# Layer-norm statistics by one product with a constant matrix, and attention that forms three heads' scores ahead

## The chip, the cores and the metric

The kernel runs on one core of one Trainium2 chip. The number that counts is the device time of one execution in microseconds (us). The engines are TensorE (PE in the profile, with its weight loads as PEld), VectorE (DVE), ScalarE (ACT), GpSimd (POOL) and SyncE (SP); SP only issues the DMAs that bring weights in.

## What is computed

The reference is a decoder trunk of two layers over 256 tokens of width 2048, in float32: a gated short convolution with an MLP, then latent attention (16 heads, keys and values from a shared latent of 512) with an MLP, and a layer norm behind each of the four.

```python
def layer_norm(x, g, b):
    mu = jnp.mean(xf, axis=-1, keepdims=True)
    var = jnp.mean(jnp.square(xf - mu), axis=-1, keepdims=True)
    y = (xf - mu) * lax.rsqrt(var + LN_EPS) * g + b
...
    s = (einsum(qn, k_nope) + einsum(qp, k_pe)) * scale    # per head and block of 128 queries
    p = jax.nn.softmax(jnp.where(mask, s, -inf))
    return einsum(p, v)
...
        h = layer_norm(ALPHA * h + mix, ln_g[layer, 0], ln_b[layer, 0])
        h = layer_norm(ALPHA * h + sq_relu_mlp(h, ...), ln_g[layer, 1], ln_b[layer, 1])
```

## The kernel before

Activations lie with the model dimension on the 128 partitions: `xres[:, m, :]` is chunk m of 16, 128 features by 256 tokens. Weights come from HBM in pieces of 512 KB (`raw` or `w`). ACT rounds such a piece to `hi` (a cast to fp32r), DVE forms the remainder `lo<-raw,hi`, and PE multiplies by both: two products with `hi`, one with `lo`. So nearly every weight piece costs an ACT instruction of about 1.05 us and a DVE instruction of about 1.2 us besides its products.

**Layer norms.** The class `Norm` (line 379) handles the first three norms: index 0 ahead of the first MLP, 1 ahead of the attention, 2 ahead of the second MLP. The fourth norm is done token by token at the end and is not touched. `prepare` and `count` sum the chunks and their squares into `S` and `Q`, 128x256 each: what is left is a sum over the partitions. The products that follow don't wait for the norm. They are taken on the not yet normalised input (`xd`), and the result is corrected with `A` (the reciprocal standard deviation of a token) and `B` (minus mean times `A`), both spread over all partitions as 128x256. `weighted` does this correction; on DVE it shows as `t<-ps_g,ab` or `t<-ps_w,ab`. `normal(m)` makes chunk m's normalised value for the residual path: two DVE instructions `nu` and one ACT instruction.

`stats` and `finish` make `A` and `B`. Four products with `S` or `Q` as weights and one column `col` as the moving side give the mean and the mean square of 128 tokens each, with tokens on partitions (`stat`, 128x4). Eight DVE instructions on 128x2 and a square root on ACT follow (`nm`, `ve` twice, `iv`, `rt`, `ra`, `rr`, `nr`). Four PE transposes by the identity `id_t` spread the two results to `lnAB`, and two ACT copies bring them to `ab`.

**Attention.** `wide_products` (line 1168) yields the nine products of the latents and calls `finish` of norm 1 first; after each of them but the first, it makes one `normal`. `project(g, box)` makes keys (`ps_k`), values (`ps_v`), rotary queries (`ps_p`) and queries (`ps_q`) of a group of four heads, in 12 steps, and two `normal` at its end. `attend(h, box)` is one head in three steps: scores `S` with mask, maximum, exponential, sum and scaling on DVE and ACT; three transposes `tp` with a copy `pt`; the product `po` with its split into `oT`. The loop behind them alternates one step of `attention` of the group before and one step of `project` of the group that follows (for the last group, of the output projection `ps_wo`). The order of the heads' steps is fixed by hand in `attention` (line 1287). Scores lie in two PSUM buffers `S`, `tp` and `po` in one each, the probabilities of a head in one of two buffers `pr2`.

The framework orders instructions of each engine on its own; only the instructions inside the MLPs' planned part keep their program order. So the place of an instruction follows from the order in the program and from the framework's scheduler. Nearly every instruction carries line 71 of the helper that records it; the names of the tiles tell them apart.

Of the kernel before, what the change touches and what calls it, by code (L numbers as in the profile page):

```python
# [53 lines left out]
def trunk(ctx: ExitStack, tc: tile.TileContext, opening, xT, vecs, w_in, w_out, w_kv, w_q, w_uk, w_uv,  # L54
# [299 lines left out]
    for _ in range(WARM):  # L354
        tensor.matmul(warm[:, :P], ones, ones, start=True, stop=True)
    vector.memset(col[:, 0:1], 1.0 / D)
    vector.memset(col[:, 1:2], 1.0 / RK)

# [20 lines left out]
    class Norm:  # L379
# [3 lines left out]
        def __init__(self, idx, scale):  # L383
            self.idx, self.scale = idx, scale
            self.S = act.tile([P, T], F32, tag="S", name=f"S{idx}")
            self.Q = act.tile([P, T], F32, tag="Q", name=f"Q{idx}")
            self.mu0 = act.tile([P, T], F32, tag="mu0", name=f"mu0{idx}") if idx != 1 else None
            self.ws = None

        def means(self):  # L390

            ps = psum("mu0c")
            for t in range(2):
                tensor.matmul(ps[:, t:t + 1], xres[:, 0, t * P:(t + 1) * P], ones[:, 0:1], start=True, stop=True)
            self.off = small.tile([P, 2], F32, tag="nm", name="off")
            vector.tensor_scalar(self.off, ps[:, 0:2], -self.scale, None, ALU.mult)
# [42 lines left out]

        def stats(self):  # L440

            st = psum("stat")
            for j in range(2):
                for b in range(2):
                    c = st[:, 2 * j + b:2 * j + b + 1]
                    tok = slice(b * P, (b + 1) * P)
                    tensor.matmul(c, (self.S, self.Q)[j][:, tok], col[:, 0:1], start=True, stop=True)
            nm = small.tile([P, 2], F32, tag="nm", name="nm")
            vector.tensor_scalar(nm, st[:, 0:2], -1.0, None, ALU.mult)
            ve = small.tile([P, 2], F32, tag="ve", name="ve")  # L450
            vector.tensor_tensor(ve, nm, nm, ALU.mult)
            vector.scalar_tensor_tensor(ve, st[:, 2:4], LN_EPS, ve, ALU.add, ALU.subtract)
            r = small.tile([P, 2], F32, tag="rr", name="rr")
            rsqrt(r, ve)
            return nm, r

        def finish(self):
            nm, r = self.stats()
            n = small.tile([P, 2], F32, tag="nr", name="nr")
            vector.tensor_tensor(n, nm, r, ALU.mult)  # L460
            ps = psum("lnAB")
            spread(ps[:, :T], r)
            spread(ps[:, T:], n)
            ab = act.tile([P, 2 * T], F32, tag="ab", name=f"ab{self.idx}")
            scalar.copy(ab[:, :T], ps[:, :T])
            scalar.copy(ab[:, T:], ps[:, T:])
            self.A, self.B = ab[:, :T], ab[:, T:]

        def gain(self, m):
# [649 lines left out]
    with tc.tile_pool(name="att", bufs=1) as ap:  # L1119
# [35 lines left out]
        def rms(out, sqs):  # L1155

            st = psum("rstat")
            for b in range(2):
                tensor.matmul(st[:, b:b + 1], sqs[:, b * P:(b + 1) * P], col[:, 1:2], start=True, stop=True)
            ve = small.tile([P, 2], F32, tag="ve", name="rve")  # L1160
            vector.tensor_scalar(ve, st[:, 0:2], RMS_EPS, None, ALU.add)
            rsqrt(out, ve)

        csq = act.tile([P, T], F32, tag="S", name="csq")
        qsq = act.tile([P, T], F32, tag="Q", name="qsq")
        todo = iter(range(NC))

        def wide_products():
            ln.finish()
            for i in range(2 * NK + 1):  # L1170
                if i < GROUP:
                    ps = ln.ws[i][1]
                else:
                    ps = psum("ps_w")
                    mm_wide([(take(), ps)], ln.xd)
                if i:
                    ln.normal(next(todo))
                yield ps
# [27 lines left out]
        oT = [ot[:, k, :] for k in range(H)]  # L1206
        kq, vp = (array(a, F32, f"kqv{a}", NC * W) for a in ("a1", "a2"))
        k2, q2, v2 = ([r[:, o:o + 1024].rearrange("p (j t) -> p j t", j=J) for o in (b, b + 1024)]
                      for r, b, J in ((kq, 0, 4), (kq, 2048, 4), (vp, 0, 2)))
        p2 = [vp[:, o:o + 512].rearrange("p (j t) -> p j t", j=2) for o in (2048, 2560)]  # L1210
        pr2 = [vp[:, o:o + 3 * P] for o in (3072, 3456)]

        with tc.tile_pool(name="att2", bufs=2) as a2, \
                tc.tile_pool(name="paux", bufs=1, space=PS) as paux:
            def project(g, box):
# [28 lines left out]
                if g == 0:  # L1244
                    query_scale()
                for _ in range(2):
                    ln.normal(next(todo))

            def attend(h, box):
# [6 lines left out]
                for b, (at, n) in enumerate(spans):  # L1256
                    tok = slice(b * P, (b + 1) * P)
                    tensor.matmul(S[:, at:at + n], qn[:, tok], kn[:, :n], start=True, stop=False)
                    tensor.matmul(S[:, at:at + n], qp[:, tok], kp[:, :n], start=False, stop=True)
                pr = pr2[h % 2]  # L1260
                mx = small.tile([P, 2], F32, tag="mx", name="mx")
# [25 lines left out]
            def attention(g, box):  # L1287
                gens = [attend(4 * g + j, box) for j in range(4)]
                for step in range(6):
                    for j in range(3, -1, -1):  # L1290
                        if 0 <= step - j < 3:
                            next(gens[j])
                            yield

# [165 lines left out]
```

## Time and profile before

| | |
|---|---|
| median of three runs | 1992.5 us (1992.46 to 1992.79) |
| the profiled execution | 1992.93 us, its span 1991.1 us |
| granted TensorE clock, mean | 0.998 |
| PE, PEld busy | 1978.0 us (99%), 1734.7 us (87%) |
| DVE busy | 1742.3 us (88%) |
| ACT busy | 1390.7 us (70%) |
| norm 0, 1, 2: first `stat` product | 380.1, 1058 and 1321 us from the span's start |
| attention, groups 0 to 3 | from 1114.6 to 1229 us |

The time of the execution is 1.8 us over the span, which goes from the first to the last instruction. A timeline's row has the start, the duration and the instruction; an "x" behind it means that some of one kind are merged, and the bracket tells how long the engine stood idle before it and on whom it waited. The durations of PE's instructions overlap, since matmuls are pipelined: what a product costs is the distance between starts.

### The profile page before, as it was taken

The page shows a single profiled execution, that of the slowest core. Times are in us where ns is not written, and L with a number is a line of the kernel's source. Part 1 is how long each engine was busy: PE and PEld are TensorE (multiplying, and loading weights), DVE is VectorE, ACT ScalarE, POOL GpSimd, SP SyncE. Part 2 cuts the span into 40 slices and gives each one's busy share as a digit, 9 for nine tenths or more (in the row PEclk, how much of TensorE's full clock was granted, in tenths as well). Part 3 has the DMA queues.
Part 4 walks back from the last instruction along what each step waited for, and adds up shares of the span by engine and source line. Part 5 has one row for each costly group of instructions (what it writes and reads, how often), then busy time and mean ns, then how long its engine had stood idle before and what let it go on. Part 6 is the DMA issues. An engine that isn't in the chain of part 4 may idle for free.

```text
span 1991.1 us, 29733 instructions
## 1 busy us (share of the span) xinstructions
PE 1978.0 (99%) x11058; PEld 1734.7 (87%) x11058; DVE 1742.3 (88%) x2630; ACT 1390.7 (70%) x2069; POOL 2.3 (0%) x21
## 2 busy tenths in 40 slices
PE   9999999999999999999999999999999999999997
PEld 8888888988888888888889998898888888888886
DVE  7657567789999999999988978778999999999997
ACT  6444445577888788878857655557788788887871
POOL 0000000000000000000000000000000000000000
PEclk9999999999999999999999999999999999999999
DMA  9655555556666666666765543654666666666673
GB/s 333 232 184 191 190 185 195 161 162 196 204 203 207 204 202 207 203 202 206 222 210 164 159 126 118 202 169 154 201 201 205 200 208 203 203 208 201 201 249 110
DMA packets 107858, 387.39 MB, mean 195 GB/s; under 512 B 11969, under 2 KB 12737, under 8 KB 107713
## 3 DMA queue, kind: packets, MB, share of 16 engines
q1 hardware_dynamic: 107568, 385.36, 61.0%
q8 instruction: 86, 1.41, 0.3%
q14 instruction: 60, 0.48, 0.1%
q10 hardware_dynamic: 144, 0.13, 0.0%
HBM read 383.35 MB, written 2.10 MB: 194 GB/s over the span
## 4 chain that ended last, share of the span: by engine, by line
PE 95%; DVE 4%; issue 0%; ACT 0%; DVEq 0%; ACTq 0%
PE ps_m L71 31%; PE sum L71 27%; PE ps_u L71 20%; PE ps_d L71 4%; PE ps_g L71 4%; PE ps_w L71 3%; DVE lo L71 1%; PE ps_wo L71 1%; PE ps_v L71 1%; DVE ropeb L71 1%; PE S L71 1%; PE po L71 0%; DVE nu L71 0%; DVE kqva L71 0%; PE turned L71 0%
## 5 line engine op out<-in xcount | busy, mean ns | idle before, releaser
L71 DVE TENSOR_TENSOR lo<-w,hi 128x1024 fp32r<-128x1024 f32 x536 | 639.9, 1218 | 34.8 <-ACT hi L71 34.2
L71 ACT CAST hi<-w 128x1024 fp32r<-128x1024 f32 x536 | 541.3, 1059 | 68.4 <-DVE w L71 65.8
L71 DVE TENSOR_TENSOR lo<-raw,hi 128x1024 fp32r<-128x1024 f32 x278 | 333.6, 1219 | 150.2 <-PE ps_u L71 84.5
L71 PE MATMUL ps_m<-xhl,hi 128*128 128x512 f32 x1792 | 424.6, 389 | 0.0
L71 ACT CAST hi<-raw 128x1024 fp32r<-128x1024 f32 x278 | 289.6, 1050 | 163.2 <-PE ps_u L71 83.4
L71 PEld LDWEIGHTS ps_m<-xhl,hi 128*128 128x128 f32 x1792 | 336.0, 188 | 69.5
L71 PE MATMUL sum<-hi,hc 128*128 128x512 f32 x736 | 277.9, 391 | 0.0
L71 PE MATMUL sum<-lo,hc 128*128 128x512 f32 x656 | 256.5, 391 | 0.0
L71 PE MATMUL sum<-hi,ha 128*128 128x512 f32 x640 | 246.4, 389 | 0.0
L71 PEld LDWEIGHTS ps_m<-xhl,lo 128*128 128x128 f32 x1792 | 229.8, 191 | 8.7
L71 PE MATMUL ps_m<-xhl,lo 128*128 128x256 f32 x1792 | 232.5, 283 | 0.0
L71 DVE TENSOR_TENSOR w<-w,w 128x512 f32<-128x512 f32 x312 | 213.0, 683 | 0.3
L71 PE MATMUL ps_u<-xhl_a,hi 128*128 128x512 f32 x704 | 164.1, 390 | 0.0
L71 PEld LDWEIGHTS sum<-hi,hc 128*128 128x128 f32 x736 | 138.6, 188 | 26.9 <-ACT sum L71 0.8
L71 PEld LDWEIGHTS ps_u<-xhl_a,hi 128*128 128x128 f32 x704 | 130.8, 188 | 26.2
L71 PEld LDWEIGHTS sum<-hi,ha 128*128 128x128 f32 x640 | 120.2, 188 | 25.9
L71 PEld LDWEIGHTS sum<-lo,hc 128*128 128x128 f32 x656 | 123.6, 188 | 21.5
L71 ACT COPY sums<-sum 128x512 f32<-128x512 f32 x194 | 112.8, 596 | 12.3 <-PE sum L71 11.8
L71 ACT COPY sum<-sums 128x512 f32<-128x512 f32 x174 | 105.4, 606 | 0.8
L71 ACT COPY t<-ps_m 128x256 f32<-128x256 f32 x112 | 42.3, 378 | 88.0 <-PE ps_m L71 88.0
L71 ACT ACTIVATE sf<-sf 128x512 f32<-128x512 f32 x120 | 76.5, 637 | 27.3 <-DVE sf L71 27.2
L71 PE MATMUL ps_w<-xd,hi 128*128 128x258 f32 x512 | 94.0, 284 | 0.0
(201 smaller groups left out, 2781.0 us busy)
## 6 DMA issues: line engine op xcount, KB each, us to landing
w<-in_w_dram SPq DMA_DIRECT2D x224, 512.0 KB, 3.9
w<-in_w2f_dram SPq DMA_DIRECT2D x208, 512.0 KB, 4.2
raw<-in_w_in_dram SPq DMA_DIRECT2D x88, 512.0 KB, 4.5
raw<-in_w_dram SPq DMA_DIRECT2D x64, 512.0 KB, 4.5
raw<-in_w_out_dram SPq DMA_DIRECT2D x32, 512.0 KB, 4.2
raw<-in_w_o_dram SPq DMA_DIRECT2D x32, 512.0 KB, 3.9
raw<-in_w2f_dram SPq DMA_DIRECT2D x16, 512.0 KB, 4.5
row<-in_opening_dram SPq DMA_DIRECT2D x15, 384.0 KB, 4.7
```

The costliest lines, as they stand in the source:

```text
L71: ins = op(*args, **named)
```

## The change

1. `finish` no longer transposes. `S` and `Q` lie side by side in one tile `SQ`, and one product of it with the constant 128x128 matrix `col` (all entries 1/2048) gives the mean and the mean square of each token on every partition at once (`stat`, 128x512). What was done on 128x2 is now done on 128x256: on ACT a square and a square root, on DVE `vr`, the reciprocal `ir`, three steps, and two for `A` and `B`. The transposes, the tile `lnAB` and its copies are gone.
2. The RMS norms of the latents use a column of `ones` with a factor in the next instruction in place of their own column of `col`; their sums share a tile.
3. `wide_products` makes four `normal` where it made eight, and `project` three at a group's end where it made two.
4. `attention` runs the heads' steps of the groups 0 to 2 in the order 0, 1, 2, 0, 3, 1, 0, 2, 1, 3, 2, 3, so that the scores of three heads stand ahead of the first transposes; probabilities have three buffers `pr3`. The last group keeps its order.

```diff
     vector.memset(ones, 1.0 / P)
...
-    vector.memset(col[:, 0:1], 1.0 / D)
-    vector.memset(col[:, 1:2], 1.0 / RK)
+    vector.memset(col, 1.0 / D)
...
-            self.S = act.tile([P, T], F32, tag="S", name=f"S{idx}")
-            self.Q = act.tile([P, T], F32, tag="Q", name=f"Q{idx}")
+            self.SQ = act.tile([P, 2 * T], F32, tag="S", name=f"S{idx}")
+            self.S, self.Q = self.SQ[:, :T], self.SQ[:, T:]
...
-        def stats(self):
...
-                    tensor.matmul(c, (self.S, self.Q)[j][:, tok], col[:, 0:1], start=True, stop=True)
...
-            rsqrt(r, ve)
-            return nm, r
-
-        def finish(self):
-            nm, r = self.stats()
-            n = small.tile([P, 2], F32, tag="nr", name="nr")
-            vector.tensor_tensor(n, nm, r, ALU.mult)
-            ps = psum("lnAB")
-            spread(ps[:, :T], r)
-            spread(ps[:, T:], n)
+        def finish(self):
+            st = psum("stat")
+            tensor.matmul(st, col, self.SQ, start=True, stop=True)
             ab = act.tile([P, 2 * T], F32, tag="ab", name=f"ab{self.idx}")
-            scalar.copy(ab[:, :T], ps[:, :T])
-            scalar.copy(ab[:, T:], ps[:, T:])
             self.A, self.B = ab[:, :T], ab[:, T:]
+            m2, ve = (tmp.tile([P, T], F32, tag="sq", name=n) for n in ("m2", "vr"))
+            s, t = (tmp.tile([P, T], F32, tag="nu", name=n) for n in ("sd", "ir"))
+            scalar.activation(m2, st[:, :T], AF.Square)
+            vector.scalar_tensor_tensor(ve, st[:, T:], LN_EPS, m2, ALU.add, ALU.subtract)
+            scalar.activation(s, ve, AF.Sqrt)
+            vector.reciprocal(t, ve)
+            vector.tensor_tensor(t, s, t, ALU.mult)
+            vector.scalar_tensor_tensor(s, s, -0.5, t, ALU.mult, ALU.mult)
+            vector.scalar_tensor_tensor(self.A, s, 1.5, t, ALU.add, ALU.mult)
+            vector.scalar_tensor_tensor(self.B, st[:, :T], -1.0, self.A, ALU.mult, ALU.mult)
...
-                tensor.matmul(st[:, b:b + 1], sqs[:, b * P:(b + 1) * P], col[:, 1:2], start=True, stop=True)
+                tensor.matmul(st[:, b:b + 1], sqs[:, b * P:(b + 1) * P], ones[:, 0:1], start=True, stop=True)
...
-            vector.tensor_scalar(ve, st[:, 0:2], RMS_EPS, None, ALU.add)
+            vector.tensor_scalar(ve, st[:, 0:2], P / RK, RMS_EPS, ALU.mult, ALU.add)
...
-                if i:
+                if 0 < i <= 4:
                     ln.normal(next(todo))
...
-        pr2 = [vp[:, o:o + 3 * P] for o in (3072, 3456)]
+        pr3 = [vp[:, o:o + 3 * P] for o in (3072, 3456, 3840)]
...
-                for _ in range(2):
+                for _ in range((3, 3, 3, 3)[g]):
                     ln.normal(next(todo))
...
-                pr = pr2[h % 2]
+                pr = pr3[h % 3]
...
-                for step in range(6):
-                    for j in range(3, -1, -1):
-                        if 0 <= step - j < 3:
-                            next(gens[j])
-                            yield
+                for j in (0, 1, 2, 0, 3, 1, 0, 2, 1, 3, 2, 3) if g < 3 else (0, 1, 0, 2, 1, 0, 3, 2, 1, 3, 2, 3):
+                    next(gens[j])
+                    yield
```

The framework's order of each engine changes at these places. A number behind a tile's name tells its buffer apart from others of that name.

**PE at norm 0**, between the first three wide products (`ps_g`) and the fourth (`ps_w`), before:

```order
L71 MATMUL ps_g<-xd_1_2671,hi_3475 128x258
L71 MATMUL ps_g<-xd_1_2671,lo_3476 128x258
L71 MATMUL ps_g<-xd_1_2671,hi_3475 128x258
L71 MATMUL stat<-col,S_350 128x1 x2
L71 MATMUL stat<-col,Q_351 128x1 x2
L71 MATMUL ps_w<-xd_0_2668,hi_3542 128x258
L71 MATMUL ps_w<-xd_0_2668,lo_3543 128x258
...
L71 MATMUL ps_w<-xd_1_2671,lo_3549 128x258
L71 MATMUL ps_w<-xd_1_2671,hi_3548 128x258 x2
L71 MATMUL lnAB<-id_t,rr 128x128 x2
L71 MATMUL lnAB<-id_t,nr 128x128 x2
L71 MATMUL ps_w<-xd_0_2668,hi_3529 128x258
```

and with the change, at the same two places:

```order
L71 MATMUL ps_g<-xd_1_2669,hi_3473 128x258
L71 MATMUL ps_g<-xd_1_2669,lo_3474 128x258
L71 MATMUL ps_g<-xd_1_2669,hi_3473 128x258
L71 MATMUL stat<-S_349,col 128x512
L71 MATMUL ps_w<-xd_0_2666,hi_3526 128x258
L71 MATMUL ps_w<-xd_0_2666,lo_3527 128x258
...
L71 MATMUL ps_w<-xd_1_2669,hi_3532 128x258 x2
L71 MATMUL ps_w<-xd_1_2669,lo_3533 128x258
L71 MATMUL ps_w<-xd_1_2669,hi_3532 128x258
L71 MATMUL ps_w<-xd_0_2666,hi_3539 128x258
L71 MATMUL ps_w<-xd_0_2666,lo_3540 128x258
```

The statistics stay where they were, as one product of 128x512 in place of four of 128x1, and of the four transposes nothing is left.

**DVE at norm 1**, from the last sum of squares on to the first correction, before (`lo` rows are weight pieces):

```order
L71 TENSOR_SCALAR nm<-stat 128x2
L71 TENSOR_TENSOR ve<-nm 128x2
L71 SCALAR_TENSOR_TENSOR ve<-stat,ve 128x2
L71 RECIPROCAL iv<-ve 128x2
L71 TENSOR_TENSOR lo_9485<-raw_9482,hi_9484 128x1024
L71 TENSOR_TENSOR rt<-sq,iv 128x2
L71 TENSOR_TENSOR lo_9762<-raw_9759,hi_9761 128x1024
L71 SCALAR_TENSOR_TENSOR ra<-sq,rt 128x2
L71 TENSOR_TENSOR lo_9768<-raw_9765,hi_9767 128x1024
L71 SCALAR_TENSOR_TENSOR rr<-ra,rt 128x2
L71 TENSOR_TENSOR lo_9840<-raw_9837,hi_9839 128x1024
L71 TENSOR_TENSOR nr<-nm,rr 128x2
```

and with the change:

```order
L71 TENSOR_TENSOR lo_9467<-raw_9464,hi_9466 128x1024
L71 TENSOR_TENSOR lo_9728<-raw_9725,hi_9727 128x1024
L71 SCALAR_TENSOR_TENSOR vr<-stat,m_9670 128x256
L71 TENSOR_TENSOR lo_9734<-raw_9731,hi_9733 128x1024
L71 RECIPROCAL ir<-vr 128x256
L71 TENSOR_TENSOR lo_9806<-raw_9803,hi_9805 128x1024
L71 TENSOR_TENSOR ir<-sd,ir 128x256
L71 TENSOR_TENSOR lo_9812<-raw_9809,hi_9811 128x1024
L71 SCALAR_TENSOR_TENSOR sd<-sd,ir 128x256
L71 SCALAR_TENSOR_TENSOR ab_9669<-sd,ir 128x256
L71 SCALAR_TENSOR_TENSOR ab_9669<-stat,ab_9669 128x256
L71 TENSOR_TENSOR t<-ps_g,ab_9669 128x256 x2
```

Before, `t<-ps_g,ab` is the next row but waits for the transposes and the copies; with the change it follows `B` on DVE itself. One more weight piece stands ahead of it.

**PE in group 1**, where the scores `S` of heads 4 to 7 stand between the key products `ps_k` of the group that follows; before, from the second head's scores on:

```order
L71 MATMUL S_10887<-kqva_10246 128x256
L71 MATMUL S_10887<-kpe,kqva_10247 128x256
L71 MATMUL ps_k<-lat,lo_10530 128x256
...
L71 MATMUL ps_k<-lat,hi_10529 128x256 x2
L71 MATMUL ps_k<-lat,lo_10636 128x256
L71 MATMUL ps_k<-lat,hi_10635 128x256 x2
L71 MATMUL tp<-id_t,kqva_10247 128x128
L71 MATMUL ps_k<-lat,lo_10636 128x256
...
L71 MATMUL ps_k<-lat,hi_10635 128x256 x2
L71 MATMUL S_10937<-kqva_10246 128x128
```

and with the change:

```order
L71 MATMUL S_10844<-kq 128x256
L71 MATMUL S_10844<-kpe,vp 128x256
L71 MATMUL ps_k<-lat,lo_10483 128x256
...
L71 MATMUL ps_k<-lat,hi_10482 128x256 x2
L71 MATMUL S_10874<-kq 128x128
L71 MATMUL S_10874<-kpe,vp 128x128
...
L71 MATMUL ps_k<-lat,lo_10599 128x256
L71 MATMUL ps_k<-lat,hi_10598 128x256 x2
L71 MATMUL tp<-id_t,vp 128x128 x3
L71 MATMUL ps_k<-lat,lo_10599 128x256
L71 MATMUL ps_k<-lat,hi_10598 128x256 x2
```

The first transposes `tp` stood one key product of 12 and three more behind the second head's scores; now the third head's scores and 24 products of `ps_k` stand between.

More of the change, by code (lines that the diff above doesn't have):

```diff
@@ L394, in means @@
                 tensor.matmul(ps[:, t:t + 1], xres[:, 0, t * P:(t + 1) * P], ones[:, 0:1], start=True, stop=True)
-            self.off = small.tile([P, 2], F32, tag="nm", name="off")
+            self.off = small.tile([P, 2], F32, tag="nr", name="off")
             vector.tensor_scalar(self.off, ps[:, 0:2], -self.scale, None, ALU.mult)
@@ L438, in wide @@
             vector.scalar_tensor_tensor(x[:, W:W + T], d, g, x[:, :T].bitcast(F32), ALU.mult, ALU.subtract)
-        def stats(self):
+        def finish(self):
             st = psum("stat")
[L443 to L446, printed above, removed]
-                    tensor.matmul(c, (self.S, self.Q)[j][:, tok], col[:, 0:1], start=True, stop=True)
[L448 to L453, printed above, removed]
-            rsqrt(r, ve)
-            return nm, r
-        def finish(self):
-            nm, r = self.stats()
-            n = small.tile([P, 2], F32, tag="nr", name="nr")
-            vector.tensor_tensor(n, nm, r, ALU.mult)
-            ps = psum("lnAB")
-            spread(ps[:, :T], r)
-            spread(ps[:, T:], n)
+            tensor.matmul(st, col, self.SQ, start=True, stop=True)
             ab = act.tile([P, 2 * T], F32, tag="ab", name=f"ab{self.idx}")
-            scalar.copy(ab[:, :T], ps[:, :T])
-            scalar.copy(ab[:, T:], ps[:, T:])
             self.A, self.B = ab[:, :T], ab[:, T:]
+            m2, ve = (tmp.tile([P, T], F32, tag="sq", name=n) for n in ("m2", "vr"))
[8 more added lines that the diff above has]
+            vector.scalar_tensor_tensor(self.B, st[:, :T], -1.0, self.A, ALU.mult, ALU.mult)
         def gain(self, m):
@@ L1158, in rms @@
             for b in range(2):
-                tensor.matmul(st[:, b:b + 1], sqs[:, b * P:(b + 1) * P], col[:, 1:2], start=True, stop=True)
+                tensor.matmul(st[:, b:b + 1], sqs[:, b * P:(b + 1) * P], ones[:, 0:1], start=True, stop=True)
             ve = small.tile([P, 2], F32, tag="ve", name="rve")
-            vector.tensor_scalar(ve, st[:, 0:2], RMS_EPS, None, ALU.add)
+            vector.tensor_scalar(ve, st[:, 0:2], P / RK, RMS_EPS, ALU.mult, ALU.add)
             rsqrt(out, ve)
-        csq = act.tile([P, T], F32, tag="S", name="csq")
-        qsq = act.tile([P, T], F32, tag="Q", name="qsq")
+        sqs = act.tile([P, 2 * T], F32, tag="S", name="csq")
+        csq, qsq = sqs[:, :T], sqs[:, T:]
         todo = iter(range(NC))
@@ L1206, in trunk @@
         oT = [ot[:, k, :] for k in range(H)]
-        kq, vp = (array(a, F32, f"kqv{a}", NC * W) for a in ("a1", "a2"))
+        kq, vp = array("a1", F32, "kq", NC * W), array("a2", F32, "vp", 4224)
         k2, q2, v2 = ([r[:, o:o + 1024].rearrange("p (j t) -> p j t", j=J) for o in (b, b + 1024)]
```

## The prediction

> **What bounds the kernel now.** I read the page's head and the chain that ended last, then the waits of PE's weight loads, and then the timelines at the places that the change touches.
>
> ```profile
> span 1991.1 us, 29733 instructions
> PE 1978.0 (99%) x11058; PEld 1734.7 (87%) x11058; DVE 1742.3 (88%) x2630; ACT 1390.7 (70%) x2069; POOL 2.3 (0%) x21
> PE 95%; DVE 4%; issue 0%; ACT 0%; DVEq 0%; ACTq 0%
> ```
>
> PE is busy for 99% of the span and makes up 95% of the chain. So only two things can shorten the run: products that PE need no longer do, and waits of PE that go. What DVE or ACT save or pay counts where PE waits for them. The waits of the weight loads (us in total, times, the longest), over the whole span:
>
> ```profile
> PEld tp L71 <- DVE kqva L71: 1.4, 4, 0.6
> PEld po L71 <- DVE oT L71: 1.2, 5, 0.3
> ...
> PEld tp L71 <- ACT oT L71: 0.9, 3, 0.3
> ...
> PEld ps_v L71 <- DVE kqva L71: 0.4, 1, 0.4
> ...
> PEld lnAB L71 <- DVE rr L71: 0.3, 1, 0.3
> PEld sum L71 <- DVE t L71: 0.3, 1, 0.3
> ```
>
> These rows hold all waits that the change could remove: 3.5 us in the attention's transposes and `po`, 0.4 at `ps_v`, 0.3 at `lnAB`, 0.3 behind norm 0. To them comes what PE does for the norms. The gain is therefore a few us of 1992.5 at best, close to what a measurement of this kernel can tell from no change (0.2%, or 4.0 us).
>
> **Norms on PE.** The timeline of norm 0, with the start and duration of each row:
>
> ```profile
> 380.00 0.28 PE L71 MATMUL ps_g<-xd,hi 128*128 128x258 f32 x1
> 380.13 0.50 PE L71 MATMUL stat<-col,S 128*128 128x1 f32 x4
> 380.49 0.58 PE L71 MATMUL stat<-col,Q 128*128 128x1 f32 x4
> 380.94 0.37 PE L71 MATMUL ps_w<-xd,hi 128*128 128x258 f32 x1
> 381.14 0.28 PE L71 MATMUL ps_w<-xd,lo 128*128 128x258 f32 x1
> ...
> 386.32 0.40 PE L71 MATMUL ps_w<-xd,hi 128*128 128x258 f32 x2
> 386.79 0.43 PE L71 MATMUL lnAB<-id_t,rr 128*128 128x128 f32 x2
> 387.06 0.38 PE L71 MATMUL lnAB<-id_t,nr 128*128 128x128 f32 x2
> 387.19 0.36 PE L71 MATMUL ps_w<-xd,hi 128*128 128x258 f32 x1
> 387.39 0.28 PE L71 MATMUL ps_w<-xd,lo 128*128 128x258 f32 x1
> ```
>
> One 128x258 product costs 0.12 us from start to start (381.14 to the next is such a step, and the pair at 386.32 another two). From 380.00 to 381.14 there are two of them besides the statistics: 1.14 - 0.24 = **0.90 us** for four products of one column, each with a weight load of its own. From 386.32 to 387.39 there are three: 1.07 - 0.36 = **0.71 us** for the four transposes, 0.27 of it the wait for `rr`.
>
> The new product is float32, 128x512. Its nearest row is the float32 product of 128x256 with `ones` as weights:
>
> ```profile
> 1207.46 0.59 PE L71 MATMUL mu0p<-xres,ones 128*128 128x256 f32 x2
> 1207.89 0.39 PE L71 MATMUL S<-kqva 128*128 128x128 f32 x2
> ```
>
> It is recorded as two passes and takes 0.43 us to the next start. Twice the columns give 0.86 us. So the statistics cost what they cost before (0.90), and the gain is the transposes: 0.75 us at norm 0. At the norms 1 and 2 no wait for `rr` stands in the list (it has one), so that 0.71 - 0.27 + 0.04, about 0.5 us each, is left. Sum: **-1.7 us** (-1.4 if the product is dearer by its 0.1 us each, -2.0 if breaking up the stream costs more at norm 1). These are PE instructions gone, hence time gone, if nothing that follows is late.
>
> **What follows the norms on DVE.** The order shows eight 128x2 instructions replaced by seven of 128x256 with a dependent chain from `vr` to `B`. What they cost, by form, in the stretch from norm 1 to the end of the attention:
>
> ```profile
> L71 DVE TENSOR_TENSOR nu<-xres,ab 128x256 f32<-128x256 f32 x16 | 6.5, 418 | 0.1
> ...
> L71 DVE SCALAR_TENSOR_TENSOR t<-ab,wgb,t 128x256 f32<-128x256 f32 x9 | 4.1, 478 | 0.0
> ...
> L71 DVE RECIPROCAL su<-su 128x2 f32<-128x2 f32 x16 | 2.6, 163 | 2.0 <-ACT kqva L71 1.7
> ...
> L71 DVE TENSOR_TENSOR mx<-mx,nsc 128x2 f32<-128x2 f32 x16 | 2.4, 153 | 0.2
> ```
>
> A two-input instruction of 128x256 takes 0.42 us and a `scalar_tensor_tensor` 0.48; their rows overlap, so that a step is 0.33 and 0.40. A reciprocal of 128x256 is nowhere in the trace. On 128x2 it takes 163 ns where a multiplication takes 153. If this difference is a fixed cost, it takes 0.43 us at 128x256; if it comes from the two elements, 5 ns each, it takes 0.42 + 256 x 0.005 = 1.7 us. Single rows differ by up to 7 ns per element, which makes 2.2 us. I take 1.7, since the slope is what the nearest row shows, and keep 0.43 and 2.2.
>
> The Trainium skill speaks against the change here: "VectorE: DVE Perf Modes", section "First, the fixed hardware budget", says that the reciprocal runs as an iterative divide with a repeat count of 8. At one repeat per cycle of the 0.96 GHz that the Trainium skill's page "Trainium Kernel Development and Optimization" gives VectorE (section "NeuronCore Architecture"), 256 elements would take an estimated 2.1 us; the rows on 128x2 can't tell that from 1.7. By it the sum below would be 0.3 us worse.
>
> Where does this land? At norms 0 and 2 nothing waits for it soon: of the corrections `t` PE waits for one alone, for 0.3 us in the list above, some 24 us behind norm 0's first `t`. The first `t` comes later by 0.3 us plus the reciprocal (the small rows and the wait for the copies go, seven larger steps come), but the order now has two weight pieces (1.15 us each) and four `nu` (0.33) fewer, 3.6 us, between it and that one: no loss up to a reciprocal of 3.3 us. At norm 1 the wait to watch is this one:
>
> ```profile
> 1065.38 0.76 DVE L71 TENSOR_TENSOR t<-ps_g,ab 128x256 f32<-128x256 f32 x2 [0.93 <-ACT ab L71]
> ...
> 1099.58 0.74 DVE L71 TENSOR_TENSOR kqva<-ps_k,rk 128x256 f32<-128x256 f32 x2
> ...
> 1099.40 0.40 PE L71 MATMUL ps_k<-lat,hi 128*128 128x256 f32 x2
> 1100.04 0.50 PE L71 MATMUL ps_v<-hi,lat 128*128 128x512 f32 x1 [0.24 <-DVE kqva L71]
> ...
> 1070.00:1098.00 28.00, 28.00 (x236) 28.00 (x236) 27.64 (x58) 22.16 (x43) 0.00 (x0) 1.00 0.55 170
> ...
> 1145.00:1175.00 30.00, 29.70 (x206) 27.41 (x205) 23.51 (x55) 17.30 (x37) 0.00 (x0) 1.00 0.39 121
> ```
>
> (The last two rows are windows: their bounds, their length, busy time of PE, PEld, DVE and ACT.) From 1070 to 1098 DVE is busy for 27.64 of 28 us: it runs behind, and the first keys leave PSUM late at 1099.58, so that `ps_v` starts 0.64 us behind the last pair of `ps_k` where 0.12 x 2 would do: a stall of about 0.4, with the refill 0.5. Norm 1 before took 6.5 us from the statistics to `t`, with 4 weight pieces among the small rows. Now there are 5 pieces of 1.15 and 1.9 us of steps, 7.7 us, plus the reciprocal. So `t` starts later by 1.2 us plus the reciprocal, less what fits into DVE's former wait for the statistics. But between `t` and the keys there is one piece (1.15 us) less, and four normalisations less, which moved to the groups where DVE has 6.5 us to spare in 30: 8 x 0.33 = 2.7 us. So the keys move by 1.2 + 1.7 - 1.15 - 2.7 = -0.95 us, while PE comes 0.5 to 0.7 earlier itself. The stall shrinks by about 0.3: **-0.3 us** (-0.5 for a reciprocal of 0.43, +0.1 for one of 2.2).
>
> ACT: a square and a root of 128x256 take the place of two copies of that size, with one table change as before. ACT is busy for 22 of 28 us there and PE waits for it nowhere in the list: nothing. The RMS norms' edit and the constants change operands, not counts: nothing.
>
> **The attention.** The first stall of group 1 and what is behind it:
>
> ```profile
> 1144.96 0.39 PE L71 MATMUL S<-kqva 128*128 128x128 f32 x2
> ...
> 1150.58 0.40 PE L71 MATMUL ps_k<-lat,hi 128*128 128x256 f32 x2
> 1151.10 0.33 PE L71 MATMUL tp<-id_t,kqva 128*128 128x128 f32 x1
> 1151.18 0.36 PE L71 MATMUL ps_k<-lat,lo 128*128 128x256 f32 x1
> 1151.38 0.28 PE L71 MATMUL ps_k<-lat,hi 128*128 128x256 f32 x1
> ...
> 1150.76 0.55 DVE L71 TENSOR_SCALAR kqva<-kqva,su 128x128 f32<-128x128 f32 x2
> ```
>
> PE has nothing left at 1150.58 + 2 x 0.12 = 1150.82 and starts the transposes at 1151.10, while DVE is scaling the probabilities: 0.28 us. The next product comes 0.20 behind instead of 0.12: 0.08 more. Now the third head's scores (1.3 us, eight passes that begin like the first row here) and nine more `ps_k` of 0.12 us stand ahead of the transposes: they are due 5.86 + 1.3 + 1.1 = 8.25 us behind the first scores in place of 5.86, and are ready at 6.14. This stall goes. DVE's own order up to the scaling is the same there.
>
> ```profile
> PEld tp L71 <- DVE kqva L71: 0.3, 1, 0.3
> PEld tp L71 <- ACT oT L71: 0.3, 1, 0.3
> PEld po L71 <- DVE oT L71: 0.3, 1, 0.3
> ```
>
> These are the waits of group 1 alone (1145 to 1175 us); group 2 has the same three. The second is the fourth head's transposes: its scores now come two slots earlier, some 5.5 us, where 0.3 lack. The third is the third head's `po`, which waits until DVE has split the one before it behind the rotary work; in the new order that split stands ahead of the last rotary sum, 0.2 to 0.3 us before PE needs it. So a group gains 0.28 + 0.28 + 0.21 and three refills of 0.08, 1.0 us; with a chance that the last stays, I count 0.95, **-1.9 us** for both (-2.0 to -0.8, if only the two transposes' waits shrink by half).
>
> Group 0 is another matter. Its first transposes wait 0.6 us, since DVE still has the query norm and late normalisations in front, and the new order puts the third head's mask ahead of the scaling. That wait stays, and only the fourth head's goes: **-0.35 us** (0 to -0.9). Group 3 keeps its order and its small waits. SP's and POOL's orders are unchanged, so no transfer moves past another.
>
> **The sum**, against the profiled execution: 1992.93 - 1.7 - 0.3 - 1.9 - 0.35 = 1988.7. The profiled execution is 0.4 above the median of 1992.5. So I predict **1988.3 us**, -4.2 us; with the terms' bounds 1986.9 to 1991.3.
>
> **Rivals.**
> 1. *The waits move instead of going.* `tp` and `po` have one PSUM tile each, and four heads share one DVE. If the steps that follow are late by what was saved, half of the attention's gain is left: -1.1 in place of -2.25, about 1989.5. For it: all waits are 0.3 us, so that 0.3 us of disorder on DVE brings one back. Against it: DVE has 6.5 us of slack in a group.
> 2. *Only the products go:* DVE backlog at norm 1 and the larger group 0 eat the rest; 1992.5 - 1.7 = 1990.8. For it: DVE at 99% there, three more passes of 128x256.
> 3. *VectorE becomes the bound behind a norm.* If the reciprocal is longer than I think, what it exceeds 1.7 by is a stall at `ps_v` (1070 to 1098 has no slack), and above 3.3 us also one at the corrections behind norms 0 and 2. The run is slower by over 0.2% only when 4.2 + 4.0 us are eaten: x - 1.7 + 2 (x - 3.3) = 8.2 gives a reciprocal of x = 5.5 us, and a time of 1996.5. The rows at 128x2 speak against it: 5.5 us are 20 ns per element, which two elements would show as 193 ns, not 163.
> 4. *Better than forecast:* group 0's wait goes too, and the reciprocal is short: -5.6 us, 1986.9.
>
> **How the numbers follow.** The forecast (1987.3 to 1989.3) gets 0.50, rival 1 0.22, rival 2 0.14, rival 3 with slower outcomes 0.06, rival 4 0.08. Faster by over 0.2% means below 1988.5: rival 4 and about three quarters of the forecast's lot, 0.45. Slower than 1996.5: 0.06. Within 0.2%: 0.49. The range of 8 in 10 takes the forecast, rivals 1 and 4 and half of rival 2: 1986.7 to 1991.2.
>
> **What the next profile would show.** `stat` with one row of some 0.86 us per norm and no `lnAB`. The row of `ir` gives the reciprocal: above 2.2 us my terms at norm 1 are wrong. The first `ps_v` should follow `ps_k` without a wait; a wait there above 0.5 is rival 3. No `tp` wait in groups 1 and 2, one of 0.4 to 0.6 in group 0; waits of `tp` or `po` of 0.2 or more in groups 1 and 2 are rival 1. Wrong altogether would be a new wait outside these stretches, in the MLPs.

## The result and the profile after

| | before | changed |
|---|---|---|
| median of 21 runs | 1992.52 us (1991.78 to 1992.98) | 1989.36 us (1988.95 to 1990.09) |
| ratio | | 0.9985, 95% interval 0.998 to 0.9991 |
| span of the profiled execution | 1991.1 us | 1987.3 us |

The change saves about 3.2 us, 0.15%: less than the 0.2% that the prediction took as the bound, and inside its range of 1986.7 to 1991.2. The interval leaves no doubt that it is faster.

The waits of PE's weight loads over the whole span of the changed kernel (us in total, times, the longest), as in the prediction's first list:

```profile
PEld po L71 <- DVE oT L71: 2.2, 5, 0.6
PEld warm L71 <- DVE ones L71: 1.0, 1, 1.0
PEld ps_w L71 <- issue: 1.0, 4, 0.2
PEld sum L71 <- ACT sum L71: 0.8, 2, 0.4
PEld tp L71 <- DVE vp L71: 0.7, 1, 0.7
```

Of the transposes' seven waits for VectorE and ScalarE one is left; the waits at `ps_v` and `lnAB` and the one of `sum` for `t` behind norm 0 are gone. The four waits of `ps_w` are new: they are the weight loads right behind the new product and belong to its price. But the wait of `po` for VectorE's split `oT` has grown from 1.2 to 2.2 us. PE's timeline at norm 0, where before stood four `stat` products and, 6 us later, four transposes:

```profile
379.00 0.28 PE L71 MATMUL ps_g<-xd,hi 128*128 128x258 f32 x1
379.12 1.02 PE L71 MATMUL stat<-S,col 128*128 128x512 f32 x2
379.58 0.68 PE L71 MATMUL ps_w<-xd,hi 128*128 128x258 f32 x1
380.10 0.28 PE L71 MATMUL ps_w<-xd,lo 128*128 128x258 f32 x1
```

From 379.00 to 380.10 there are two ordinary products of 0.12 us: 1.10 - 0.24 = 0.86 us for the new product, in two passes. VectorE's rows for the same norm's tiles, which give the reciprocal (minimum, median and maximum of a duration in ns, and when the first and last started):

```profile
L71 DVE RECIPROCAL ir<-vr x3: 1742/1743/1747, 383.4 to 1322.4; 128x256 f32<-128x256 f32 x3
L71 DVE TENSOR_TENSOR ir<-sd,ir x3: 407/411/411, 386.2 to 1325.2; 128x256 f32<-128x256 f32 x3
```

The reciprocal of 128x256 takes 1.74 us, four times a multiplication of that size.

To compare the traces stage by stage, I take the start of one product from each timeline and subtract it from that of the next. "Norm 0" goes from the first `stat` to the first `sum` product, "norm 1" from its `stat` to the first `ps_k`, "keys" from there to the first `ps_v`, "values" to the first `S`, "group g" from the first `S` of a group to that of the next, "norm 2" from its `stat` to the end of the span. What lies between these agrees within 0.2 us in all kernels where nothing else is said.

| us | norm 0 | norm 1 | keys | values | group 0 | group 1 | group 2 | norm 2 | `stat` of norm 0 to the end |
|---|---|---|---|---|---|---|---|---|---|
| before | 30.47 | 35.93 | 6.24 | 14.61 | 30.31 | 30.09 | 30.03 | 669.55 | 1611.01 |
| changed | 29.73 | 35.41 | 5.84 | 14.47 | 30.49 | 29.73 | 29.72 | 669.15 | 1608.16 |
| difference | -0.74 | -0.52 | -0.40 | -0.14 | +0.18 | -0.36 | -0.31 | -0.40 | -2.85 |

So 1.66 us come from the three norms, 0.54 from the keys and values, and only 0.49 from the attention's three groups, of which the prediction expected 2.25. The other 1.0 us between the two profiled spans stands ahead of norm 0 and isn't the change's (last section).

Where the attention's gain went: group 1 of the changed kernel, PE and then VectorE.

```profile
1167.07 0.28 PE L71 MATMUL ps_q<-lat,lo 128*128 128x256 f32 x1
1167.19 0.28 PE L71 MATMUL ps_q<-lat,hi 128*128 128x256 f32 x1
1167.89 0.48 PE L71 MATMUL po<-pt,vp 128*128 128x256 f32 x1 [0.42 <-DVE oT L71]
```

```profile
1162.38 0.42 DVE L71 TENSOR_TENSOR oT<-po,oT 128x256 fp32r<-128x256 f32 x1
1162.71 0.41 DVE L71 TENSOR_TENSOR ropea<-ps_p,cos_t 128x256 f32<-128x256 f32 x1
1163.14 1.72 DVE L71 TENSOR_TENSOR ropeb<-ps_p,sin_t 32x256 f32<-32x256 f32 x4
1164.89 0.42 DVE L71 TENSOR_TENSOR ropea<-ps_p,cos_t 128x256 f32<-128x256 f32 x1
1165.23 0.42 DVE L71 TENSOR_TENSOR vp<-ropea,ropeb 128x256 f32<-128x256 f32 x1
1165.66 1.72 DVE L71 TENSOR_TENSOR ropeb<-ps_p,sin_t 32x256 f32<-32x256 f32 x4
1167.42 0.42 DVE L71 TENSOR_TENSOR oT<-po,oT 128x256 fp32r<-128x256 f32 x1
```

PE could go on at 1167.19 + 0.12 = 1167.31 and starts the third head's `po` at 1167.89, when VectorE has read the second head's: a wait of 0.58 us, where it was 0.21 before. VectorE works through the first rotary sum and the four `ropeb` of the second without a pause and reaches the split (`oT<-po,oT`) behind them.

### The profile page after: what moved, and what is told of

It is laid out like the page before. It is cut to its first block, busy times and chain, and to the rows that moved or that the text cites. A ratio compares the mean times of both kernels' runs of the same rounds, so it can differ in the third digit from the quotient of the medians.

```text
span 1987.3 us, 29678 instructions
## 1 busy us (share of the span) xinstructions
PE 1973.6 (99%) x11028; PEld 1730.7 (87%) x11028; DVE 1748.7 (88%) x2623; ACT 1389.3 (70%) x2066; POOL 2.3 (0%) x21
## 4 chain that ended last, share of the span: by engine, by line
PE 94%; DVE 4%; ACT 1%; issue 1%; DVEq 0%; ACTq 0%
PE ps_m L71 31%; PE sum L71 27%; PE ps_u L71 20%; PE ps_d L71 4%; PE ps_g L71 4%; PE ps_w L71 3%; DVE lo L71 1%; PE ps_wo L71 1%; DVE ropeb L71 1%; PE S L71 1%; PE ps_k L71 1%; PE ps_v L71 0%; DVE nu L71 0%; PE ps_q L71 0%; PE po L71 0%
```

## The experiments

Each run is the changed kernel but for what its diff says; only e2 starts from the kernel before. The number of probability buffers follows the order of heads, also where the diff leaves it out. The medians are of 11 runs, beside 33 of the kernel before on the same chip (1992.3 to 1992.5 us).

| us | median | norm 0 | norm 1 | keys | values | group 0 | group 1 | group 2 | norm 2 |
|---|---|---|---|---|---|---|---|---|---|
| changed | 1989.36 | 29.73 | 35.41 | 5.84 | 14.47 | 30.49 | 29.73 | 29.72 | 669.15 |
| e1, norms only | 1992.53 | 29.73 | 35.41 | 8.03 | 16.17 | 29.95 | 30.10 | 30.05 | 669.22 |
| e2, attention only | 1991.59 | 30.47 | 35.93 | 6.22 | 14.59 | 30.30 | 29.72 | 29.74 | 669.64 |
| e3, `po` ahead of `tp` | 1989.83 | 29.73 | 35.41 | 5.84 | 14.47 | 30.58 | 29.74 | 29.74 | 669.16 |
| e4, shared tiles too | 1987.93 | 29.73 | 35.41 | 5.84 | 14.46 | 29.87 | 29.17 | 29.17 | 669.20 |
| e5, query norm early | 1988.60 | 29.73 | 35.41 | 5.84 | 14.55 | 29.71 | 29.16 | 29.17 | 669.21 |
| e6, two reciprocals | 1992.53 | 29.73 | 37.11 | 5.83 | 14.54 | 30.60 | 29.72 | 29.74 | 669.57 |
| e7, old attention | 1990.40 | 29.73 | 35.41 | 5.84 | 14.47 | 30.60 | 30.09 | 30.03 | 669.22 |
| e8, late normalisations | 1988.36 | 29.73 | 35.41 | 5.84 | 14.47 | 29.86 | 29.17 | 29.14 | 669.18 |
| e9, none in group 0 | 1987.88 | 29.73 | 35.41 | 5.84 | 14.47 | 29.88 | 29.17 | 29.15 | 669.14 |
| e10, e5 and e9 | 1988.03 | 29.73 | 35.41 | 5.84 | 14.56 | 29.69 | 29.16 | 29.16 | 669.15 |
| e11, no reciprocal | 1989.78 | 29.73 | 35.41 | 5.84 | 14.46 | 30.79 | 29.73 | 29.72 | 669.14 |
| e12, shared tiles alone | 1987.82 | 29.73 | 35.41 | 5.84 | 14.47 | 29.89 | 29.05 | 29.05 | 669.15 |

### e1: the norms without the rest

```diff
-                if 0 < i <= 4:
+                if i:
-                for _ in range((3, 3, 3, 3)[g]):
+                for _ in range(2):
-                for j in (0, 1, 2, 0, 3, 1, 0, 2, 1, 3, 2, 3) if g < 3 else (0, 1, 0, 2, 1, 0, 3, 2, 1, 3, 2, 3):
+                for j in (0, 1, 0, 2, 1, 0, 3, 2, 1, 3, 2, 3):
```

> The norms by one product, without the other two parts: eight normalisations among the latents, two a group, the old order of heads, two probability buffers. Theory A (the reciprocal of 1.74 us is paid for by the four normalisations that the change moved away from the full stretch before ps_v): PE saves about 1.7 us at the norms, but the first keys come 1.2 + 1.74 - 1.15 = 1.8 us later on VectorE while PE is 0.5 earlier, so the wait at the first ps_v grows from 0.5 to about 2.5 us: 1992.1 to 1993.0, no gain left. Theory B (the chain behind the norm is hidden anyway): 1990.8, with a ps_v wait of 0.5 or less.

The ratio to before is 1.0001 (0.9991 to 1.001): nothing is left, as theory A had it. PE's timeline at the first `ps_v`:

```profile
1097.13 0.40 PE L71 MATMUL ps_k<-lat,hi 128*128 128x256 f32 x2
1099.56 0.50 PE L71 MATMUL ps_v<-hi,lat 128*128 128x512 f32 x1 [2.03 <-DVE kq L71]
```

The norms gain what they gain in the changed kernel, and 2.2 us are given back at the keys, where `ps_v` waits for VectorE. The move of four normalisations pays for the longer chain; theory B falls.

The values are 1.7 us longer for another reason. Windows of this run (bounds, length, busy time of PE, PEld, DVE, ACT and POOL, granted clock, DMA) and two rows of `ps_v`:

```profile
1097.00:1099.50 2.50, 0.53 (x5) 0.32 (x3) 2.50 (x6) 1.61 (x3) 0.00 (x0) 1.00 0.35 108
1101.00:1104.00 3.00, 3.00 (x9) 2.33 (x8) 3.00 (x6) 0.00 (x0) 0.00 (x0) 0.50 0.64 208
```

```profile
1102.21 1.05 PE L71 MATMUL ps_v<-hi,lat 128*128 128x512 f32 x2
1103.06 0.63 PE L71 MATMUL ps_v<-lo,lat 128*128 128x512 f32 x1
```

PE waits for nothing there, but the granted clock is 0.50, in the trace's record from 1100.69 on for 3.41 us, and a product of 128x512 takes 0.43 us from start to start where it takes 0.23 in the changed kernel: half of 3.41 us is the 1.7. PE had stood idle for 2.03 us just before, the longest idle time behind the opening in the fourteen traces, and no other trace shows such a fall between the opening and the last 9 us. One case is not enough to call the idle time the cause, but it's the likely one; e6's idle time of 1.47 us brought no fall. The profiled execution took 1993.36 us, 0.8 above the median, so the fall need not have come in all eleven; their times alone don't show it.

### e2: the attention without the rest

```diff
-                for step in range(6):
...
+                for j in (0, 1, 2, 0, 3, 1, 0, 2, 1, 3, 2, 3) if g < 3 else (0, 1, 0, 2, 1, 0, 3, 2, 1, 3, 2, 3):
+                    next(gens[j])
+                    yield
```

> The kernel before with the new order of heads and three probability buffers alone; old norms, two normalisations a group. Theory A (order: in a group the second head's split stands on VectorE behind the second rotary sum, and the third head's po waits for it): the transposes' waits go, but a po wait of 0.4 to 0.6 us stands in each of the groups 0 to 2, and a group gains 0.3: 1991.7 to 1992.2. Theory B (load: the new po wait comes from the third normalisation in each group and the reciprocal's backlog): no such wait here, a gain of 0.9 a group, 1990.0 to 1990.6.

Groups 1 and 2 take what they take in the changed kernel, and its list of waits has the same three waits of `po` for VectorE:

```profile
PE po L71 <- DVE oT L71: 1.2, 3, 0.4
PE tp L71 <- DVE vp L71: 0.3, 1, 0.3
```

The median lies 0.1 us below theory A's range, the gain of a group is theory A's. So neither the third normalisation of a group nor the reciprocal makes the new wait. It belongs to the order of heads itself. (The interval of the whole, 0.9987 to 1.0004, takes in no change; the stages tell more.)

### e3: the second head's po ahead of the third head's transposes

```diff
-                for j in (0, 1, 2, 0, 3, 1, 0, 2, 1, 3, 2, 3) if g < 3 else (0, 1, 0, 2, 1, 0, 3, 2, 1, 3, 2, 3):
+                for j in (0, 1, 2, 0, 3, 1, 0, 1, 2, 3, 2, 3) if g < 3 else (0, 1, 0, 2, 1, 0, 3, 2, 1, 3, 2, 3):
```

> The changed kernel with one exchange in the order of heads: the second head's po one step earlier, ahead of the third head's transposes (0, 1, 2, 0, 3, 1, 0, 1, 2, 3, 2, 3). Its split then stands ahead of the second rotary sum on VectorE. Theory A: the po wait of 0.6 us goes in each of the groups 0 to 2, 1.9 us in all: 1987.3 to 1987.8. Theory B: the wait stays or moves to the next step: 1989.1 to 1989.6.

1989.83 us: theory A's number was wrong. The split of the second head does come ahead of the second rotary sum, but the groups stay at 29.74 us. The wait has split up and moved, to the second head's `po` (in the framework's order it stands behind 23 products of `ps_p` in place of 12 in e4, and starts right behind the first head's split, which follows two weight pieces) and to the last head's:

```profile
1171.54 0.28 PE L71 MATMUL ps_q<-lat,lo 128*128 128x256 f32 x1
1171.96 0.92 PE L71 MATMUL po<-pt,vp 128*128 128x256 f32 x4
```

Here 0.42 us pass where 0.12 would do. Of the two orders, each only decides which `po` waits.

### e4: e3, and tp and po share two tiles

```diff
-                tp = paux.tile([P, 512], F32, tag="ta", name="tp")
+                tp = paux.tile([P, 512], F32, tag="ta", name="tp", bufs=2)
-                po = paux.tile([P, 512], F32, tag="tb", name="po")
+                po = paux.tile([P, 512], F32, tag="ta", name="po", bufs=2)
```

> As e3, and tp and po share two PSUM tiles instead of having one each, so that a po no longer waits for the split of the po before it. Theory A: no po wait is left even where VectorE is late; 1987.2 to 1987.8. If e3 has settled the wait, the same as e3 within 0.3. Theory B (VectorE's load): transposes now wait for splits, 1989 or more.

1987.93 us, 0.1 above theory A's range, and groups of 29.17: PE waits for no `oT` any more in this kernel's list. The price is small: the last group, with the old order, gets 0.2 us longer, where a `po` now waits for ScalarE's `pt` (up to 0.5 in e5, e8 and e10).

### e5, e8, e9 and e10: what holds group 0

All four start from e4: e5 adds the first diff, e8 the second, e9 the third, and e10 the first and the third:

```diff
                 w = take()
                 for b in range(2):
...
+                if g == 0:
+                    query_scale()
                 w = take(1)
...
-                if g == 0:
-                    query_scale()
```

```diff
-                if 0 < i <= 4:
+                if 0 < i <= 2:
-                for _ in range((3, 3, 3, 3)[g]):
+                for _ in range((2, 4, 4, 4)[g]):
```

```diff
-                for _ in range((3, 3, 3, 3)[g]):
+                for _ in range((0, 4, 4, 4)[g]):
```

> e4 with the query norm of the latents taken ahead of the rotary queries of group 0 in place of behind its queries; all else as in e4. Theory A (the first transposes of group 0 wait, 0.7 us in e4, because the query norm's chain with its table change on ScalarE and the late normalisations stand ahead of the first head's exponentials): the wait goes, 1987.1 to 1987.4. Theory B (VectorE is simply behind from the norm on, and the chain only fills the time): the wait stays within 0.2 us, 1987.8 to 1988.1.

> e4 with two normalisations among the latents in place of four, and 2, 4, 4 and 4 in the groups. Theory A (VectorE's load ahead of group 0): 1.35 us less ahead of the first transposes of group 0, whose wait of 0.7 us goes; groups 1 and 2, with 7 us of VectorE to spare, stay at 29.2: 1987.1 to 1987.4. Theory B (the chain of the query norm sets it): the wait stays, 1987.8 to 1988.1.

> e4 with no normalisation at group 0's end and 4 at the ends of the groups 1 to 3. Theory A (e5 and e8 left group 0 at 29.7 to 29.9 us since in both VectorE still has normalisation steps and weight pieces between the first head's mask and its scaling; those of group 0's end fall right there): group 0 takes 29.2 to 29.5 us, 0.4 to 0.6 less than in e4. Theory B (weight pieces alone make it late): 29.8 to 29.9 us, no change to e4.

> e9 with the query norm early as in e5. Theory A: group 0 takes 29.2 us like the groups 1 and 2 of e4, and the whole 0.5 to 0.7 us less than e4. Theory B: as e5, 29.7 us.

Group 0 stays at 29.69 to 29.88 us in all four, as each theory B had it; the medians of e5 and e8 lie above both of their ranges. The early query norm takes 0.2 us off, the moved normalisations nothing. But the runs with fewer of these did not take out what they were meant to, as VectorE's timeline of e10 shows, between the second head's mask and the first head's scaling:

```profile
1118.56 0.41 DVE L71 TENSOR_TENSOR nu<-xres,ab 128x256 f32<-128x256 f32 x1
1118.89 0.60 DVE L71 TENSOR_REDUCE mx<-vp 128x1 f32<-128x128 f32 x2
1119.42 0.41 DVE L71 TENSOR_TENSOR kq<-ps_k,rk 128x256 f32<-128x256 f32 x1
1119.75 0.15 DVE L71 TENSOR_TENSOR mx<-mx,nsc 128x2 f32<-128x2 f32 x1
1119.82 0.42 DVE L71 TENSOR_TENSOR nu<-nu,ab 128x256 f32<-128x256 f32 x1
1120.15 0.42 DVE L71 TENSOR_TENSOR nu<-xres,ab 128x256 f32<-128x256 f32 x1
1120.49 0.16 DVE L71 RECIPROCAL su<-su 128x2 f32<-128x2 f32 x1
1120.56 0.54 DVE L71 TENSOR_TENSOR vp<-S,mask_t 128x384 f32<-128x384 f32 x1
1121.02 0.54 DVE L71 TENSOR_SCALAR vp<-vp,su 128x128 f32<-128x128 f32 x2
```

Normalisation steps `nu` still stand there, though no normalisation is called at this group's end: the framework has put others into the place. In group 1 of the changed kernel none stands there, and the third head's mask follows the scaling. So the query norm is not the cause, or only 0.2 us of it; whether the normalisation steps, the mask or the weight pieces ahead of them are, these runs can't tell, and it stays open. The medians of the four lie within 0.7 us of e4, no more than single runs of a kernel differ by.

### e6 and e11: two reciprocals and none

```diff
+            vector.reciprocal(t, ve)
             vector.reciprocal(t, ve)
```

```diff
-            vector.reciprocal(t, ve)
+            vector.tensor_scalar(t, ve, 0.25, None, ALU.mult)
```

> The changed kernel with each of the three norms' reciprocals taken twice, 1.74 us more on VectorE a norm, the result the same. Theory A (norm 1 has some 0.4 us of room at the first ps_v, the norms 0 and 2 have room up to a reciprocal of 3.3 us): a ps_v wait of about 1.2 us, a little more in group 0, next to nothing at the norms 0 and 2: 1990.6 to 1991.3. Theory B (what stands behind a norm on VectorE is hidden): 1989.2 to 1989.6. Theory C (the room at the norms 0 and 2 is overrated): 1992 or more, with waits of PE 20 to 35 us behind these norms.

> The changed kernel without the reciprocal of the three layer norms: a multiplication by a constant of the same size (0.28 us) stands in its place, so that the normalised values are others. Theory A (the reciprocal of 1.74 us fits just into the room that VectorE has behind each norm): 1989.2 to 1989.6, no gain, the stages at the norms as in the changed kernel within 0.1 us. Theory B (it costs at one of the norms or at ps_v): 1988.0 to 1988.9, and that stage is shorter.

Without the reciprocal the stages at the norms and the keys are the same to 0.01 us: its 1.74 us cost nothing there in the changed kernel. (Group 0 is 0.30 longer, with a wait of 1.0 at `tp` where it was 0.7, and the median is 0.2 above theory A's range; why isn't shown.) With two, all 3.2 us of the change are gone again (ratio 1.0001, 0.9991 to 1.001). That is more than theory A's 1.2 to 1.9, and at another place; theory C had the number, but most of the loss is at norm 1. PE's timeline at norm 1:

```profile
1070.06 0.36 PE L71 MATMUL ps_w<-xd,hi 128*128 128x258 f32 x1 [1.47 <-DVE t L71]
```

and the waits of its weight loads between 370 and 420 us, behind norm 0:

```profile
PEld sum L71 <- DVE t L71: 0.8, 1, 0.8
```

At norm 1 the wide products stop first, not `ps_v`: they go through the PSUM tiles in turn, and the next one is free only when VectorE has taken the first correction `t` out of it. The stage grows by 1.70 us, the whole second reciprocal. Behind norm 0 the wait for `t` that I took to be covered is back, and the time from the first `sum` product to norm 1 grows from 647.16 to 647.83 us. The stage of norm 2 is 0.42 longer, but not by a wait for `t`: the 0.42 us are a wait of `sum` for ScalarE at 1449.5 us, some 130 us behind the norm (0.8 us of the weight load, 0.4 in the changed kernel), and that the reciprocal causes it is not shown. So norm 1 has room for one reciprocal and for hardly anything more.

### e7: the changed kernel with the old attention

```diff
-                for j in (0, 1, 2, 0, 3, 1, 0, 2, 1, 3, 2, 3) if g < 3 else (0, 1, 0, 2, 1, 0, 3, 2, 1, 3, 2, 3):
+                for j in (0, 1, 0, 2, 1, 0, 3, 2, 1, 3, 2, 3):
-        pr3 = [vp[:, o:o + 3 * P] for o in (3072, 3456, 3840)]
+        pr2 = [vp[:, o:o + 3 * P] for o in (3072, 3456)]
```

> The changed kernel with the old order of heads and two probability buffers: norms by one product, and the normalisations moved. Theory A: 1.65 us at the norms and 0.4 to 0.5 at ps_v, the groups take 30.3, 30.1 and 30.0 us as before: 1990.1 to 1990.6. Theory B (three normalisations a group crowd VectorE): the waits of the transposes grow, groups of 30.3 us and more, 1990.8 to 1991.5.

As theory A had it. The norms and the moved normalisations are worth 1992.4 - 1990.4 = 2.0 us, the order of heads another 1.0. Groups 1 and 2 take exactly what they took before, with three normalisations each: VectorE's load there is no matter. Only group 0 is 0.3 longer.

### e12: the shared tiles in the change's own order

```diff
-                tp = paux.tile([P, 512], F32, tag="ta", name="tp")
+                tp = paux.tile([P, 512], F32, tag="ta", name="tp", bufs=2)
-                po = paux.tile([P, 512], F32, tag="tb", name="po")
+                po = paux.tile([P, 512], F32, tag="ta", name="po", bufs=2)
```

> The changed kernel in its own order of heads, with tp and po sharing two PSUM tiles: tp and po take turns, so that a po falls on the tile of the po before it from the second head on. Theory A (what holds a po is the tile of the po before, not read by VectorE yet): this order keeps that for the third head's po, so the wait of 0.4 to 0.6 us stays and the groups 1 and 2 take 29.7 us; e4 needed order and tiles together. Theory B (the second tile alone does it): 29.2 us, 1988 like e4.

Theory A's number was wrong again: 1987.82 us, with groups 1 and 2 at 29.05, the shortest of all. I had counted the tiles out by turns; the trace shows that the third head's `po` doesn't wait for the second's split, so it doesn't get the tile of the one before. PE first, then VectorE:

```profile
1166.62 0.40 PE L71 MATMUL ps_q<-lat,hi 128*128 128x256 f32 x2
1166.86 0.82 PE L71 MATMUL po<-pt,vp 128*128 128x256 f32 x4
```

```profile
1165.44 1.72 DVE L71 TENSOR_TENSOR ropeb<-ps_p,sin_t 32x256 f32<-32x256 f32 x4
1167.19 0.42 DVE L71 TENSOR_TENSOR oT<-po,oT 128x256 fp32r<-128x256 f32 x1
```

VectorE's order is that of the changed kernel, and the split is as late as there: it begins at 1167.19. But PE starts the third head's `po` at 1166.86 without a wait and ahead of that split. (The framework also puts it two products of `ps_q` earlier: 12 stand ahead of it since the last transposes, 14 in the changed kernel.) A group is 29.73 - 29.05 = 0.68 us shorter, the wait of 0.58 and a refill of 0.1. This settles the cause: `po` has its operands in time, and a single PSUM tile makes it wait for VectorE's split. Against the kernel before, e12 has a ratio of 0.9978 (0.9969 to 0.9987): with e4 and e9 the fastest version here, and two lines more than the change.

## Why the prediction held, and where it did not

The predicted time, 1988.3 us, was 1.1 us too low; the likeliest of the rivals against it, that the waits move, is what happened.

- **Norms on PE: right.** Predicted -1.7 us, measured 0.74 + 0.52 + 0.40 = 1.66. The new product was put at 0.86 us from the row of 128x256 and takes 0.86; norm 0 was put at 0.75 and gives 0.74, the norms 1 and 2 at 0.5 each and give 0.52 and 0.40.
- **The reciprocal: right.** The slope from 128x2 gave 1.7 us; the row says 1.74. The estimate from the Trainium skill's repeat count ("VectorE: DVE Perf Modes", section "First, the fixed hardware budget"), 2.1 us, was 0.4 too high; that the operation iterates agrees with the row, 1.74 us for 256 elements where a multiplication takes 0.41.
- **The keys: right in mechanism.** Predicted -0.3 us, measured -0.40, and 0.14 in the values. e1 shows that without the four moved normalisations the chain costs 2.2 us at the keys. (The change has six VectorE instructions of 128x256 in a norm, not seven; the sum's 1.9 us of steps are the right five beside the reciprocal.)
- **The room behind the norms: mis-sized.** The prediction's "no loss up to a reciprocal of 3.3 us" at the norms 0 and 2 was counted from VectorE's rows alone and left out that PE itself comes 0.74 us earlier. In the changed kernel the `t` behind norm 0 for which PE could wait ends at 409.93, and PE is at its product at 410.93: 1.0 us are left, so the room is 1.74 + 1.0 = 2.7 us, and two reciprocals (3.5 us) cost 0.7 there. At norm 1 I looked at `ps_v` alone; the PSUM tiles of the wide products run out first, by 1.7 us.
- **Groups 1 and 2: the step that failed.** The transposes' waits went, as predicted. The third term did not: "in the new order that split stands ahead of the last rotary sum, 0.2 to 0.3 us before PE needs it". VectorE of the kernel before, in group 1, has the split at the very place where the changed kernel has it, behind the four `ropeb` of the second rotary sum and ahead of its final addition:

```profile
1169.15 1.72 DVE L71 TENSOR_TENSOR ropeb<-ps_p,sin_t 32x256 f32<-32x256 f32 x4
1170.91 0.42 DVE L71 TENSOR_TENSOR oT<-po,oT 128x256 fp32r<-128x256 f32 x1
1171.25 0.42 DVE L71 TENSOR_TENSOR kqva<-ropea,ropeb 128x256 f32<-128x256 f32 x1
```

So the new order brought no change there. Counted from the group's first score product (1144.96 before, 1142.21 now), VectorE begins the split at 25.2 us where it took 25.95, a gain of 0.7; PE reaches the third head's `po` 25.1 us behind it where it took 26.2, a gain of 1.1. Of PE's gain 0.7 are the transposes' waits and refills, and 0.36 are three products of `ps_q` that the framework now puts behind this `po`: 17 stood between the last transposes and it, now 14. Those 0.36 us are not saved, and they come out as PE's longer wait: 0.58 - 0.21 = 0.37. So a group gains 0.28 + 0.28 + 2 x 0.08 from the transposes and loses 0.37 at `po`: 0.35 by these terms, 0.36 and 0.31 by the stages, instead of 0.95. This is what rival 1 describes, and its time of 1989.5 us was nearer than the forecast.
- **Group 0: wrong sign.** Predicted -0.35, measured +0.18: its first transposes still wait (0.7 us), and the same `po` wait came on top. e12 takes the latter away (29.89 us). What holds the transposes is open.

The sum with the measured terms: 1992.93 - 1.66 - 0.54 - 0.49 leaves 1990.2 for the profiled execution; the whole of 2.85 us from `stat` to the end includes some 0.15 in the stretches between, most of it from norm 0 to norm 1 (647.28 before, 647.16 now), where the wait for `t` stood that the prediction had listed as removable.

## What to carry to other kernels

Where a wait is removed ahead of an engine that runs in order, recompute the next wait with PE's new arrival time, and see in both orders what stands ahead of it: where PE arrives earlier by more than the engine that feeds it, the wait moves one step on. If a product waits for another engine to read its PSUM tile, try a second tile before another order: here it was worth 0.68 us a group, the exchange of order nothing. A longer chain on an engine can be free (1.74 us here) as long as work of the same size can be moved out of the full stretch behind it; ask for the first buffer that runs out, not only for the engine that is named in the present wait. And read the granted clock before a stage is explained by waits: 1.7 us of e1 were the clock's.

## What was not expected of the hardware

The opening of the program is the same up to norm 0 in all kernels but for a constant's fill, yet the first `stat` product of norm 0 came at 379.1 to 380.1 us in the fourteen profiles; e2, whose opening is that of the kernel before (380.1), has it at 379.1. PE's timeline of the kernel before, of the changed kernel and of e3 at the first weight pieces:

```profile
5.34 2.02 PE L71 MATMUL ps_g<-xhl_a,hifirst 128*128 128x512 f32 x4
7.19 0.64 PE L71 MATMUL ps_g<-xhl_a,lofirst 128*128 128x256 f32 x4
```

```profile
5.17 1.15 PE L71 MATMUL ps_g<-xhl_a,hifirst 128*128 128x512 f32 x4
6.16 0.64 PE L71 MATMUL ps_g<-xhl_a,lofirst 128*128 128x256 f32 x4
```

```profile
5.34 1.94 PE L71 MATMUL ps_g<-xhl_a,hifirst 128*128 128x512 f32 x4
7.12 0.64 PE L71 MATMUL ps_g<-xhl_a,lofirst 128*128 128x256 f32 x4
```

The same four products take 1.85 us in one execution and 0.99 in the other; e3, which opens as the changed kernel does, takes 1.78. In the traces' records the granted clock is full from 7.19, 4.66 and 7.02 us on in these three, which is where the products get faster: 0.43 us a product of 128x512 before, 0.23 after. (The profile's windows show 1.00 ahead of that moment too, where the trace has no record.) The Trainium skill ("TensorE: Matmul & The Clock Gate", section "What's actually happening") says that the array's clock is at half for the first 3.4 us of work and that the window which releases it runs freely, so that the moment varies from run to run. The rows agree that it varies: PE's first product starts at 1.05 us in all fourteen traces, and the full clock comes between 3.92 and 7.19, after 2.9 to 6.1 us of work. Not all of the scatter is the clock's: e4 has the full clock from 5.59 on and its `stat` at 379.88, e12 from 5.83 on and 379.50. For a change of 3 us this scatter of 1 us matters: single executions can't be compared by their spans, only from a product behind the opening, or by medians of many runs.
